# First transfers, first modulation column and planner margins of a fused transformer block, changed together

## The chip, the core and the metric

The kernel runs on one core of a Trainium2 chip. The core has a matrix engine (PE, which multiplies a 128x128 stationary tile with a moving tile of up to 512 columns), a vector engine (DVE), an activation engine (ACT), a general engine (POOL), and transfers that SP issues (DMA). The engines run side by side and wait for each other through semaphores. The metric is the device time of one execution in microseconds (us).

## The reference

One block works on x (1024 tokens of 1024 features) with a conditioning vector c, all in float32. Cut to what is computed:

```python
c_act = silu(c)
shift1, scale1, gate1, shift2, scale2, gate2 = split(c_act @ ada_w + ada_b, 6)
h = rmsnorm(x, norm1_g) * (1 + scale1) + shift1
u, v, val, gate = split(h @ w_in + b_in, 4)            # 512 columns each
y_a = gelu(u) * (causal_mix_in_chunks_of_128(layernorm(gelu(v))) + b_s)
y_b = silu(group_layernorm(causal_conv31(val * sigmoid(gate))))
x = x + gate1 * (concat(rmsnorm(y_a), rmsnorm(y_b)) @ w_out)
h2 = rmsnorm(x, norm2_g) * (1 + scale2) + shift2
g, up = split(h2 @ w_ffn_in, 2)                        # 2816 columns each
x = x + gate2 * ((silu(g) * up) @ w_ffn_out)
shift_f, scale_f = split(c_act @ ada_f_w + ada_f_b, 2)
out = rmsnorm(x, norm_f_g) * (1 + scale_f) + shift_f
```

## The kernel before

Features lie on the 128 partitions and tokens along the rows, so a feature block k (0 to 7) of x is a tile of 128 x 1024. The tokens are worked in two halves of 512. A product in float32 is made from three products of parts: each operand is split into a high part of shorter numbers and a low part with the rest, and `mm3` adds high x high (L750), low weight x high (L751) and high weight x low (L752). The high part is a copy by ACT and the low part a subtraction on DVE or POOL (L733 and L734 turn a weight `raw_k` into `wh_k` and `wl_k`). The FFN forms its products from seven sums of blocks (L1131 to L1139).

The columns of the modulation (scale, shift and gate; 64 columns of 128 features) are products of a 128 x 1024 piece of `ada_w` with silu(c), which stands in every partition of `cact`. DVE multiplies and sums a piece in one instruction (L703, SCALAR_TENSOR_TENSOR over 1024 elements, its sum read out behind it); some pieces go over POOL and ACT instead (L700, L701). `cact` is made at the start: PE spreads c over the partitions (L662), ACT takes silu (L663).

The start makes the norm's factor for the first half. As the blocks of x land, `first_rstd` squares them (L886 on DVE for odd k, L888 on ACT for even k), PE sums over the features (L890), ACT takes the root (L894), DVE the reciprocal (L895), and four matmuls with `sel_tok` spread the factors over the partitions (L897). `keep_busy` puts matmuls on a tile of zeros, `idle`, between these steps (L876). Then, for each k: two columns (scale, shift), the weight `wk[k]`, the scaled x `t_h` (L926), its modulated high part `h` (L928, ACT) and low part (L932, L933), and 24 products into eight PSUM tiles. The columns' pieces land in the tiles `ypad`, which the convolution uses later.

Behind that, for the first half: the products of u, v and the gated values (`glu`, L826); the convolution of 31 taps on DVE and POOL (`conv_pair`: `cv` at L1070 and L1073, its sum with POOL's part `s` at L1079); the chunk mixing, whose bias tile is `bst` (L860, from row sums `rs` that PE makes in a PSUM tile); the norms of both branches (`rt_a`, `rt_b`, L799); and w_out. The second half follows with the same steps, then the FFN, and last the final norm (L1442).

The order of instructions on each engine isn't that of the code. `fix_order` builds a graph of all steps with a cost for each, lists it forward by rank and backward, several times, and binds each engine to the resulting order. It makes 12 such orders (three pairs of factors by which steps and transfers are stretched, four rounds each) and keeps the one that `replay` finds best over jittered costs. `edges` are order constraints given by hand; one list of them holds the transfers of the first phase (`in_turn`).

## Time and profile before

| quantity | value |
| --- | --- |
| median of 3 runs | 964.54 us (963.92 to 966.73) |
| profiled execution | 967.9 us, its span 965.8 us |
| PE busy | 946.5 us (98%) |
| DVE busy | 861.9 us (89%) |
| ACT busy | 482.1 us (50%) |
| POOL busy | 413.6 us (43%) |
| granted clock of PE, mean | 0.995 |
| PE busy in the first 20 us | 15.03 us |
| PE busy from 120 to 140 us | 18.30 us, granted clock 0.91 |
| PE busy in the last 26 us | 16.69 us |

In the timeline a row has the start, the duration, the engine, the line, the operation, the tiles, and in brackets the idle time of the engine before it with what ended it. A row of several instructions has their number behind x and their whole time. In the list of waits a row names who waited, for whom, the total in us, the times and the longest. Matmuls overlap, so the time from one start to the next tells the pace of PE.

### The profile page before, as it was taken

To read this page: it belongs to the slowest core of one execution; us is meant where nothing else is said; L and a number is where in the kernel's file an instruction comes from. 1 tells how busy PE (TensorE), PEld (TensorE's weight loads), DVE (VectorE), ACT (ScalarE), POOL (GpSimd) and SP (SyncE) were. 2 spreads that over 40 slices of the span, in tenths; PEclk is the share of its full clock that TensorE was granted. 3 is DMA by queue.
4 is the path that set the end of the run, shared out by engine and by line. 5 is a ranking of instruction groups with operands and counts; after the bars stand their busy time and mean duration, and the time that the engine had idled before them with its cause. 6 is when DMAs were issued, how large, how long until landed. Compare 5 with 4: busy or idle time off the path is not lost.

```text
span 965.8 us, 12863 instructions
## 1 busy us (share of the span) xinstructions
PE 946.5 (98%) x4461; PEld 767.1 (79%) x4461; DVE 861.9 (89%) x1226; ACT 482.1 (50%) x770; POOL 413.6 (43%) x253
## 2 busy tenths in 40 slices
...
GB/s 351 325 265 136 110 174 88 153 159 130 139 280 202 147 146 138 263 205 119 239 238 251 221 236 243 249 236 238 224 171 277 269 158 260 164 33 165 54 1 174
DMA packets 70498, 184.24 MB, mean 191 GB/s; under 512 B 7841, under 2 KB 8353, under 8 KB 70434
## 3 DMA queue, kind: packets, MB, share of 16 engines
...
## 4 chain that ended last, share of the span: by engine, by line
PE 84%; DVE 9%; DMA 2%; ACT 2%; issue 2%; POOL 1%; SPq 0%; POOLq 0%; ACTq 0%; DVEq 0%
PE B L1139 31%; PE C L1139 18%; PE ah L1139 9%; PE A L1139 3%; PE po L752 3%; PE po L751 3%; PE po L750 3%; DVE cv L1070 2%; PE p L752 2%; PE p L750 2%; PE p L751 2%; PE v L750 2%; PE v L752 1%; DVE ada L703 1%; PE v L751 1%
## 5 line engine op out<-in xcount | busy, mean ns | idle before, releaser
L1139 PE MATMUL B<-h,w_f 128*128 128x512 f32 x816 | 189.9, 389 | 0.6 <-ACT w_f L1131 0.3
L1139 PEld LDWEIGHTS B<-h,w_f 128*128 128x128 f32 x816 | 153.1, 188 | 33.0 <-ACT w_f L1131 0.8
L1070 DVE SCALAR_TENSOR_TENSOR cv<-ypad,colt,cv 128x512 f32<-128x512 f32 x216 | 147.8, 745 | 0.3
L1139 PE MATMUL B<-fa,w_d 128*128 128x512 f32 x528 | 125.0, 389 | 0.0
L1139 PE MATMUL C<-h,w_f 128*128 128x512 f32 x528 | 123.7, 389 | 0.0
L1139 PEld LDWEIGHTS C<-h,w_f 128*128 128x128 f32 x528 | 99.1, 188 | 20.9 <-ACT w_f L1131 0.3
L1139 PEld LDWEIGHTS B<-fa,w_d 128*128 128x128 f32 x528 | 99.0, 188 | 20.9 <-DVE x L1500 0.3
L1139 PE MATMUL ah<-h,wh_a 128*128 128x512 f32 x320 | 101.3, 394 | 0.0
L1426 POOL TENSOR_TENSOR sq_nf<-sq_nf,sq_nf 128x512 f32<-128x512 f32 (+1 forms) x15 | 17.4, 1163 | 170.9 <-ACT sq_nf L1420 170.8
L1131 ACT ACTIVATE w_f<-raw_f 128x512 fp32r<-128x512 f32 x68 | 42.4, 630 | 87.8 <-PE B L1139 38.8
L734 POOL TENSOR_TENSOR wl_a<-raw_a,wh_a 128x1024 fp32r<-128x1024 f32 x20 | 49.4, 2468 | 77.0 <-ACT wh_a L733 77.0
L1131 ACT ACTIVATE w_d<-raw_d 128x512 fp32r<-128x512 f32 (+1 forms) x72 | 42.0, 593 | 80.2 <-PE B L1139 33.6
L1132 DVE TENSOR_TENSOR w_f<-raw_f,w_f 128x512 fp32r<-128x512 f32 x68 | 71.7, 1061 | 7.6 <-ACT w_f L1131 7.4
L1139 PEld LDWEIGHTS ah<-h,wh_a 128*128 128x128 f32 x320 | 59.8, 188 | 14.8 <-issue 1.7
L1383 POOL TENSOR_TENSOR x<-x,up 128x512 f32<-128x512 f32 x20 | 36.1, 1805 | 73.4 <-ACT x L1382 73.4
L1139 PE MATMUL C<-fa,w_d 128*128 128x512 f32 (+1 forms) x291 | 63.9, 370 | 0.0
L1139 PE MATMUL ah<-h,wl_a 128*128 128x512 f32 x160 | 62.3, 389 | 0.0
L1139 PEld LDWEIGHTS C<-fa,w_d 128*128 128x128 f32 x291 | 51.0, 188 | 9.2
L1132 DVE TENSOR_TENSOR fa<-a,fa 128x512 fp32r<-128x512 f32 x77 | 52.0, 712 | 1.1 <-ACT fa L1131 1.1
L1500 DVE SCALAR_TENSOR_TENSOR x<-B,cond,x 128x512 f32<-128x512 f32 x48 | 35.7, 746 | 18.0 <-PE B L1139 17.5
L1132 DVE TENSOR_TENSOR w_d<-raw_d,w_d 128x512 fp32r<-128x512 f32 (+1 forms) x72 | 50.6, 712 | 0.0
L1131 ACT ACTIVATE fa<-a 128x512 fp32r<-128x512 f32 x77 | 46.5, 626 | 7.4 <-DMA a<-acts 4.8
...
## 6 DMA issues: line engine op xcount, KB each, us to landing
...
```

What stands on the lines that cost most here:

```text
L703: V.scalar_tensor_tensor(raw, raw, 1.0, cact, op0=ALU.mult, op1=ALU.mult, accum_out=cond[:, j:j + 1])
L734: lo_eng.tensor_tensor(lo[:, cut], raw[:, cut], hi[:, cut].bitcast(F32), op=ALU.subtract)
L750: PE.matmul(acc, shi, mhi, start=start, stop=False)
L751: PE.matmul(acc, slo, mhi, start=False, stop=False)
L752: PE.matmul(acc, shi, mlo, start=False, stop=stop)
L1070: V.scalar_tensor_tensor(accs[j], src, wc, accs[j], op0=ALU.mult, op1=ALU.add)
L1131: A.activation(dst[:, 0, :], src, AF.Copy)
L1132: lo_eng.tensor_tensor(dst[:, 1, :], src, dst[:, 0, :].bitcast(F32), op=ALU.subtract)
L1139: last_mm = PE.matmul(bank[:, cols], s, m[:, cols], start=first and p == 0 and i == 0, stop=p == n - 1 and i == 2, skip_group_check=True)
L1383: G.tensor_tensor(g0, g0, up0, op=ALU.mult)
L1426: G.tensor_tensor(run, run, t, op=ALU.add)
L1500: V.scalar_tensor_tensor(x_tile(k, part), bank[:, cols], ccol(GATE2, k), x_tile(k, part), op0=ALU.mult, op1=ALU.add)
```

## The change

At the start it does the following.

- The transfers' order is pair 0 of x's blocks, c, the first 80 columns of the small constants `colt` (with c as eight columns in it), pairs 1 and 2, pair 3 as two halves, then the matrix for the first scale column, the piece for the first shift column, `wk[0]` in two halves, and the rest of `colt`. Before it was c, the four pairs, the two pieces, `wk[0]`, `colt`.
- The first scale column is made by PE: eight matmuls with the columns of silu(c) as stationary operand, a copy by ACT, and one matmul that sums the rows. The DVE step for it falls away.
- `gain` (one plus the bias, times the norm's gain) is made right after the first square instead of behind the first `t_h`.
- The squares of k = 1, 3, 4, 5 and 7 are on DVE, those of 0, 2 and 6 on ACT.
- The first `h` is made by DVE (TENSOR_SCALAR) instead of ACT.
- Ten matmuls on `idle`, 128x512, are added (nine stand ahead of the c matmuls in the order that comes out); the ones between the steps are now 32x128 and more of them (`IDLE`).
- The first steps of DVE, ACT and the transfers are bound to the written order by `edges`.

In the planner, the replay falls away. One pair of factors, (1.03, 1.1), two rounds, and ranks with a random term replace the 12 orders. With this the order moves a little in the whole program.

```diff
-IDLE = (1, 1, 2, 3, 3)
+IDLE = (4, 6, 6, 6, 4)
+WARM_UP = 10
+BY_VECTOR = (1, 3, 4, 5, 7)
...
-MARGINS = ((1.01, 1.05), (1.015, 1.075), (1.02, 1.1))
-JITTER = (0.008, 0.08)
-TRIALS = 4
+MARGIN = (1.03, 1.1)
+ROUNDS_OF_ORDER, SPREAD, SEED = 2, 0.05, 577509
...
-def jittered(g, order, seed):
+def fix_order(tc, edges, stacked, reusing):
 
     import random
-    rng = random.Random(seed)
-    with stretched(g, lambda s: 1 + abs(rng.gauss(0, JITTER[s.dma]))):
-        return replay(g, order)
-
-
-def fix_order(tc, edges, stacked, reusing, rounds=4):
-
+    rng = random.Random(SEED)
     g = Graph(list(tc.nc.cur_bb.bb.instructions), edges, stacked, reusing)
-    orders = []
-    for margin in MARGINS:
-        with stretched(g, lambda s: margin[s.dma]):
-            order, done, follows = forward(g, list(range(len(g.steps))))
-            for _ in range(rounds):
-                tail = backward(g, [-t for t in done], follows)
-                order, done, follows = forward(g, [-t for t in tail])
-                orders.append(order)
-    times = [sum(jittered(g, order, seed) for seed in range(TRIALS)) for order in orders]
-    best = orders[times.index(min(times))]
-    for steps in best.values():
+    with stretched(g, lambda s: MARGIN[s.dma]):
+        order, done, follows = forward(g, list(range(len(g.steps))))
+        for _ in range(ROUNDS_OF_ORDER):
+            tail = backward(g, [-t for t in done], follows)
+            order, done, follows = forward(g, [-(t + rng.gauss(0, SPREAD)) for t in tail])
+    for steps in order.values():
...
-    c_load = nc.sync.dma_start(c_row[0:1, :], c).ins
     colt = const.tile([P, NCOL], F32, name="colt")
     xs = [[const.tile([P, 2, H], F32, name=f"x{half}_{i}") for i in range(KD // 2)] for half in range(2)]
-    in_turn = [c_load] + [nc.sync.dma_start(xs[0][i], xT[0, i]).ins for i in range(KD // 2)]
+    early = _OFF["norm2_g"]
+    in_turn = [nc.sync.dma_start(xs[0][0], xT[0, 0]).ins, nc.sync.dma_start(c_row[0:1, :], c).ins,
+               nc.sync.dma_start(colt[:, 0:early], cols[:, 0:early]).ins]
+    in_turn += [nc.sync.dma_start(xs[0][i], xT[0, i]).ins for i in range(1, KD // 2 - 1)]
+    in_turn += [nc.sync.dma_start(xs[0][KD // 2 - 1][:, a, :], xT[0, KD // 2 - 1, :, a, :]).ins for a in range(2)]
...
+    cact_cols = colt[:, 0:KD]
+    A.activation(cact_cols, cact_cols, AF.Silu)
+    silu, on = [], dict(V=[], A=[])
     for h in range(2):
         cb = cv_bank(f"c{h}")
         PE.matmul(cb, ones[0:1].broadcast_to([1, P]), c_row[0:1, hs(h)], start=True, stop=True)
-        silu = A.activation(cact[:, hs(h)], cb, AF.Silu).ins
-    with issue_after(silu):
+        silu.append(A.activation(cact[:, hs(h)], cb, AF.Silu).ins)
+    with issue_after(silu[-1]):
...
-        nc.sync.dma_start(raw, src)
+        for i in range(parts):
+            cut = slice(i * 1024 // parts, (i + 1) * 1024 // parts)
+            nc.sync.dma_start(raw[:, cut], src[:, cut])
...
-            ins = PE.matmul(first_bank(3, 0), idle[:, 0:P], idle, start=True, stop=True).ins
+            ins = PE.matmul(first_bank(3, 0)[0:32, 0:P], idle[:, 0:32], idle[:, 0:P], start=True, stop=True).ins
...
-            if k % 2:
-                V.tensor_tensor(t, src, src, op=ALU.mult)
+            if k in BY_VECTOR:
+                on["V"].append(V.tensor_tensor(t, src, src, op=ALU.mult).ins)
             else:
-                A.activation(t, src, AF.Square)
+                on["A"].append(A.activation(t, src, AF.Square).ins)
+                if k == 0:
+                    on["A"] += silu
             for q in range(4):
                 mm = PE.matmul(bank[q * 32:(q + 1) * 32, 0:P], ones.broadcast_to([P, 32]),
                                t[:, q * P:(q + 1) * P], start=k == 0, stop=k == KD - 1).ins
             keep_busy(IDLE[k // 2] if k % 2 else 0, mm)
         rt = sb.tile([P, P], F32, tag="rt", name="rt_n1_0", bufs=2)
-        A.activation(rt, bank[:, 0:P], AF.Sqrt, bias=epst, scale=1.0 / D)
+        on["A"].append(A.activation(rt, bank[:, 0:P], AF.Sqrt, bias=epst, scale=1.0 / D).ins)
         last["rstd"] = V.reciprocal(rt, rt).ins
+        on["V"].append(last["rstd"])
         for q in range(4):
             mm = PE.matmul(bank[:, q * P:(q + 1) * P], sel_tok[:, q:q + 1].broadcast_to([P, P]),
                            rt, start=True, stop=True).ins
         keep_busy(IDLE[4], mm)
         return bank
 
+    for _ in range(WARM_UP):
+        PE.matmul(first_bank(3, 0), idle[:, 0:P], idle, start=True, stop=True)
     r1a_bank = first_rstd()
...
     gain = const.tile([P, KD], F32, name="gain")
+    V.scalar_tensor_tensor(gain, bcol(SCALE1, 0, KD), 1.0, colt[:, _OFF["norm1_g"]:_OFF["norm1_g"] + KD],
+                           op0=ALU.add, op1=ALU.mult)
+
+    def first_scale():
+
+        raw = ypad[0][:, HALO:HALO + D]
+        nc.sync.dma_start(raw, ada1)
+        bank = gn_bank("scale_rows")
+        for k in range(KD):
+            q = k % 4
+            PE.matmul(bank[q * 32:(q + 1) * 32, 0:P], cact_cols[:, k:k + 1].broadcast_to([P, 32]),
+                      raw[:, k * P:(k + 1) * P], start=k < 4, stop=k >= 4)
+        rows = sb.tile([P, P], F32, tag="rt", name="scale_rows", bufs=2)
+        on["A"].append(A.activation(rows, bank[:, 0:P], AF.Copy).ins)
+        PE.matmul(bank[:, P:P + 1], rows, sel_tok[:, 4:5], start=True, stop=True)
+        return bank[:, P:P + 1]
+
     for k in range(KD):
         n = len(nc.cur_bb.bb.instructions)
-        ada_cols(SCALE1 * 8 + k, dst=ypad[2 * k % 4][:, HALO:HALO + D])
-        with issue_after(last["rstd"]):
+        if k == 0:
+            first_scale_col = first_scale()
+        else:
+            ada_cols(SCALE1 * 8 + k, dst=ypad[2 * k % 4][:, HALO:HALO + D])
+        with issue_after(last["rstd"]) if k else nullcontext():
             ada_cols(SHIFT1 * 8 + k, dst=ypad[(2 * k + 1) % 4][:, HALO:HALO + D])
+        if k == 0:
+            behind = len(nc.cur_bb.bb.instructions)
+            t = tmp("t_h1_0_0")
+            on["V"].append(V.tensor_tensor(t, x_tile(0, hs(0)), r1a_bank, op=ALU.mult).ins)
         w_k = weights(wk[k], f"k{k}", V, parts=2 if k == 0 else 1)
-        scale, shift, weight = loads(n)
+        in_turn += loads(n)
         if k == 0:
-            in_turn += [scale, shift, weight, nc.sync.dma_start(colt, cols).ins]
-            V.scalar_tensor_tensor(gain, bcol(SCALE1, 0, KD), 1.0, colt[:, _OFF["norm1_g"]:_OFF["norm1_g"] + KD],
-                                   op0=ALU.add, op1=ALU.mult)
+            in_turn.append(nc.sync.dma_start(colt[:, early:], cols[:, early:]).ins)
+        scaled = A.activation(ccol(SCALE1, k), first_scale_col if k == 0 else ccol(SCALE1, k), AF.Identity,
+                              bias=gain[:, k:k + 1], scale=col("norm1_g", k)).ins
+        shifted = A.activation(ccol(SHIFT1, k), ccol(SHIFT1, k), AF.Identity, bias=bcol(SHIFT1, k)).ins
+        if k:
+            t = tmp(f"t_h1_0_{k}")
+            V.tensor_tensor(t, x_tile(k, hs(0)), r1a, op=ALU.mult)
+        h = h1[0][k] = act_tile(f"h1_0_{k}", 0)
+        if k == 0:
+            h_hi = V.tensor_scalar(h[:, 0, :], t, ccol(SCALE1, k), ccol(SHIFT1, k), op0=ALU.mult, op1=ALU.add).ins
         else:
-            in_turn += [scale, shift, weight]
-        A.activation(ccol(SCALE1, k), ccol(SCALE1, k), AF.Identity, bias=gain[:, k:k + 1], scale=col("norm1_g", k))
-        A.activation(ccol(SHIFT1, k), ccol(SHIFT1, k), AF.Identity, bias=bcol(SHIFT1, k))
-        t = tmp(f"t_h1_0_{k}")
-        V.tensor_tensor(t, x_tile(k, hs(0)), r1a_bank if k == 0 else r1a, op=ALU.mult)
-        h = h1[0][k] = act_tile(f"h1_0_{k}", 0)
-        h_hi = A.activation(h[:, 0, :], t, AF.Identity, bias=ccol(SHIFT1, k), scale=ccol(SCALE1, k)).ins
+            h_hi = A.activation(h[:, 0, :], t, AF.Identity, bias=ccol(SHIFT1, k), scale=ccol(SCALE1, k)).ins
         if k == 0:
-            with issue_after(h_hi):
-                A.activation(r1a, r1a_bank, AF.Copy)
+            on["V"].append(h_hi)
+            kinds = [[i for i in nc.cur_bb.bb.instructions[behind:] if i.engine == e and type(i).__name__ != "InstDMACopy"]
+                     for e in (nc.vector.engine, nc.scalar.engine)]
+            on["V"] += [i for i in kinds[0] if i not in on["V"]]
+            rounded = [i for i in kinds[1] if i not in (scaled, shifted)]
+            on["A"] += [scaled, *rounded[:1], shifted, *rounded[1:], A.activation(r1a, r1a_bank, AF.Copy).ins]
         A.activation(t, t, AF.Identity, bias=ccol(SHIFT1, k), scale=ccol(SCALE1, k))
         V.tensor_tensor(h[:, 1, :], t, h[:, 0, :].bitcast(F32), op=ALU.subtract)
         for j in range(4):
             for vg in range(2):
                 mm3(first_bank(j, vg), unit(w_k, 4 * vg + j), full(h), k == 0, k == KD - 1)
-    edges.extend((b.name, a.name) for a, b in zip(in_turn, in_turn[1:]))
+    for ins in (in_turn, on["V"], on["A"]):
+        edges.extend((b.name, a.name) for a, b in zip(ins, ins[1:]))
```

DVE at the start, before. `ypad` rows are columns (the first is the scale of k = 0, the second its shift), `wl_k` is the low part of a weight, and the last row is the low part of `h` of k = 0.

```order
L886 TENSOR_TENSOR sq_n_0_7_171<-x_3_78 128x512
L703 SCALAR_TENSOR_TENSOR ypad_108,cond<-ypad_108,cact 128x1024
L895 RECIPROCAL rt_n_0_180<-rt_n_0_180 128x128
L703 SCALAR_TENSOR_TENSOR ypad_109,cond<-ypad_109,cact 128x1024
L926 TENSOR_TENSOR t_h_0_0_208<-x_0_75,ssq_n_0_123 128x512
L919 SCALAR_TENSOR_TENSOR gain<-colt 128x8
L734 TENSOR_TENSOR wl_k_199<-raw_k_196,wh_k_198 128x512 x2
L703 SCALAR_TENSOR_TENSOR ypad_110,cond<-ypad_110,cact 128x1024
L933 TENSOR_TENSOR h_0_0_210<-t_h_0_0_208,h_0_0_210 128x512
```

DVE there, after:

```order
L850 TENSOR_TENSOR sq_n_0_7_200<-x_3_77 128x512
L861 RECIPROCAL rt_n_0_212<-rt_n_0_212 128x128
L665 SCALAR_TENSOR_TENSOR ypad_116,cond<-ypad_116,cact 128x1024
L907 TENSOR_TENSOR t_h_0_0_241<-x_0_74,ssq_n_0_141 128x512
L920 TENSOR_SCALAR h_0_0_255<-t_h_0_0_241,cond 128x512
L698 TENSOR_TENSOR wl_k_247<-raw_k_243,wh_k_246 128x512 x2
L931 TENSOR_TENSOR h_0_0_255<-t_h_0_0_241,h_0_0_255 128x512
```

The scale column and `gain` are gone from this stretch (`gain` stands five rows ahead of it), the first `h` (TENSOR_SCALAR) has come in, and the weight's low parts and the low part of `h` follow without a column between them.

PE in the products of k = 1, before (`h_0_1` is the block's `h`; L752 rows take its low part):

```order
L750 MATMUL p_0_215<-h_0_1_260,wh_k_252 128x512
L751 MATMUL p_0_215<-h_0_1_260,wl_k_253 128x512
L752 MATMUL p_0_215<-h_0_1_260,wh_k_252 128x512
L750 MATMUL p_1_219<-h_0_1_260,wh_k_252 128x512
L751 MATMUL p_1_219<-h_0_1_260,wl_k_253 128x512
L752 MATMUL p_1_219<-h_0_1_260,wh_k_252 128x512
L750 MATMUL p_0_223<-h_0_1_260,wh_k_252 128x512
```

PE there, after (L714, L715 and L716 are the lines L750, L751 and L752 of before):

```order
L714 MATMUL p_1_264<-h_0_1_305,wh_k_297 128x512
L714 MATMUL p_0_268<-h_0_1_305,wh_k_297 128x512
L714 MATMUL p_1_272<-h_0_1_305,wh_k_297 128x512
L715 MATMUL p_0_260<-h_0_1_305,wl_k_298 128x512
L715 MATMUL p_1_264<-h_0_1_305,wl_k_298 128x512
L715 MATMUL p_0_268<-h_0_1_305,wl_k_298 128x512
L715 MATMUL p_1_272<-h_0_1_305,wl_k_298 128x512
L714 MATMUL p_0_276<-h_0_1_305,wh_k_297 128x512
L715 MATMUL p_0_276<-h_0_1_305,wl_k_298 128x512
L714 MATMUL p_1_280<-h_0_1_305,wh_k_297 128x512
L715 MATMUL p_1_280<-h_0_1_305,wl_k_298 128x512
L716 MATMUL p_0_260<-h_0_1_305,wh_k_297 128x512
```

The low part of `h` was needed by the third product of the block; now it is needed by the 13th (one L714 row stands ahead of those shown).

DVE around `bst`, before. `ada` is a modulation column that DVE makes, `cv` are taps of the convolution, `s` the sums that close its first pair of blocks, and the `cv_2` and `cv_3` rows open the second pair.

```order
L1070 SCALAR_TENSOR_TENSOR cv_0_1214<-ypad_108,colt,cv_0_1214 128x512
L1070 SCALAR_TENSOR_TENSOR cv_1_1215<-ypad_109,colt,cv_1_1215 128x512
L1079 TENSOR_TENSOR s_0_1210<-s_0_1210,cv_0_1214 128x512
L1079 TENSOR_TENSOR s_1_1211<-s_1_1211,cv_1_1215 128x512
L1073 TENSOR_SCALAR cv_2_1530<-ypad_110,colt 128x512
L1073 TENSOR_SCALAR cv_3_1531<-ypad_111,colt 128x512
L860 SCALAR_TENSOR_TENSOR bst<-rs,colt,bst 128x128 x4
L1070 SCALAR_TENSOR_TENSOR cv_2_1530<-ypad_110,colt,cv_2_1530 128x512
L1070 SCALAR_TENSOR_TENSOR cv_3_1531<-ypad_111,colt,cv_3_1531 128x512
```

DVE there, after:

```order
L1069 SCALAR_TENSOR_TENSOR cv_1_1260<-ypad_116,colt,cv_1_1260 128x512
L1069 SCALAR_TENSOR_TENSOR cv_0_1259<-ypad_115,colt,cv_0_1259 128x512
L1069 SCALAR_TENSOR_TENSOR cv_1_1260<-ypad_116,colt,cv_1_1260 128x512
L824 SCALAR_TENSOR_TENSOR bst<-rs,colt,bst 128x128 x4
L1069 SCALAR_TENSOR_TENSOR cv_0_1259<-ypad_115,colt,cv_0_1259 128x512
L1069 SCALAR_TENSOR_TENSOR cv_1_1260<-ypad_116,colt,cv_1_1260 128x512
L1069 SCALAR_TENSOR_TENSOR cv_0_1259<-ypad_115,colt,cv_0_1259 128x512
L1069 SCALAR_TENSOR_TENSOR cv_1_1260<-ypad_116,colt,cv_1_1260 128x512
L1078 TENSOR_TENSOR s_0_1255<-s_0_1255,cv_0_1259 128x512
L1078 TENSOR_TENSOR s_1_1256<-s_1_1256,cv_1_1260 128x512
L1072 TENSOR_SCALAR cv_2_1575<-ypad_117,colt 128x512
L1072 TENSOR_SCALAR cv_3_1576<-ypad_118,colt 128x512
```

`bst` stood behind the first pair's last taps, its sums and the first taps of the next pair; now four taps of the first pair, the sums and those first taps all stand behind it.

42 lines of the change are left out of this document (6 added, 36 removed).

## Prediction

> **What bounds the kernel now.** I read the page first, then who waited for whom on PE, then the timeline of the two places where PE waits longest. PE is busy for 946.5 of 965.8 us, so whatever this change can win lies in the 19 us that are left and in stretches where the clock of PE is low.
>
> ```profile
> span 965.8 us, 12863 instructions
> PE 946.5 (98%) x4461; PEld 767.1 (79%) x4461; DVE 861.9 (89%) x1226; ACT 482.1 (50%) x770; POOL 413.6 (43%) x253
> ...
> PE c L662 <- DMA c_row<-c: 2.4, 1, 2.4
> PE v L750 <- DVE bst L860: 2.1, 1, 2.1
> ...
> PE p L750 <- ACT h L928: 1.7, 1, 1.7
> PE p L752 <- DVE h L933: 1.0, 1, 1.0
> ...
> PE pm L1013 <- DVE ya L1019: 0.8, 1, 0.8
> PE ssq_b L805 <- DVE rt_b L799: 0.6, 1, 0.6
> ```
>
> These are PE's waits (total, times, longest). The rows on c and h belong to the start, which the diff rewrites. The row on bst is a single wait in the middle, which no line of the diff names but which the new order of DVE moves. These are the start's steps in order of time (start, duration, engine, line):
>
> ```profile
> 1.01 0.27 DVE L864 MEMSET idle<- 128x256 uint32 x1
> 2.44 3.75 PE L662 MATMUL c<-c_row,ones 1*128 1x512 f32 x4 [2.44 <-DMA c_row<-c]
> 6.33 0.58 ACT L663 ACTIVATE cact<-c 128x512 f32<-128x512 f32 x1
> 6.93 1.28 ACT L665 ACT_TABLE_LOAD   x1
> ...
> 8.22 0.20 ACT L665 ACTIVATE warm<-epst 128x1 f32<-128x1 f32 x1
> 9.38 0.69 DVE L886 TENSOR_TENSOR sq_n<-x 128x512 f32<-128x512 f32 x1 [0.56 <-DMA x<-xT]
> 10.65 1.23 DVE L703 SCALAR_TENSOR_TENSOR ypad<-ypad,cact 128x1024 f32<-128x1024 f32 x1 [0.58 <-DMA ypad<-ada]
> 11.04 0.37 ACT L894 ACTIVATE rt_n<-ssq_n,epst 128x128 f32<-128x128 f32 x1 [1.04 <-PE ssq_n L890]
> 11.80 0.95 DVE L895 RECIPROCAL rt_n<-rt_n 128x128 f32<-128x128 f32 x1
> 14.00 0.69 DVE L926 TENSOR_TENSOR t_h<-x,ssq_n 128x512 f32<-128x512 f32 x1 [0.17 <-PE ssq_n L897]
> 15.41 0.81 ACT L928 ACTIVATE h<-t_h,cond 128x512 fp32r<-128x512 f32 x1
> 16.27 0.50 PE L750 MATMUL p<-h,wh_k 128*128 128x512 f32 x1 [1.66 <-ACT h L928]
> 18.86 1.89 DVE L926 TENSOR_TENSOR t_h<-x,r_n 128x512 f32<-128x512 f32 x3
> 20.67 1.22 DVE L734 TENSOR_TENSOR wl_k<-raw_k,wh_k 128x1024 fp32r<-128x1024 f32 x1
> 21.80 1.22 DVE L703 SCALAR_TENSOR_TENSOR ypad<-ypad,cact 128x1024 f32<-128x1024 f32 x1
> 22.95 0.68 DVE L933 TENSOR_TENSOR h<-t_h,h 128x512 fp32r<-128x512 f32 x1
> 23.68 0.50 PE L752 MATMUL p<-h,wh_k 128*128 128x512 f32 x1 [1.01 <-DVE h L933]
> ```
>
> What starts the real products is one chain: last part of x (9.38), square, sum, root, reciprocal (ends 12.75), t_h at 14.00, h by ACT to 16.22, PE at 16.27. The scale column's 1.23 us on DVE holds the reciprocal from 11.41 to 11.80. PE stops again at 23.68 for the low part of the second k-block; the next of these waits in time is the one for bst, near 120.
>
> The second place:
>
> ```profile
> 106.15 6.59 DVE L703 SCALAR_TENSOR_TENSOR ada<-ada,cact 128x1024 f32<-128x1024 f32 x1
> 106.90 4.76 POOL L734 TENSOR_TENSOR wl_v<-raw_v,wh_v 128x1024 fp32r<-128x1024 f32 x2
> 112.67 5.36 DVE L1070 SCALAR_TENSOR_TENSOR cv<-ypad,colt,cv 128x512 f32<-128x512 f32 x8
> 117.94 1.27 DVE L1079 TENSOR_TENSOR s<-s,cv 128x512 f32<-128x512 f32 x2
> 119.13 1.39 DVE L1073 TENSOR_SCALAR cv<-ypad,colt 128x512 f32<-128x512 f32 x2
> 120.44 1.11 DVE L860 SCALAR_TENSOR_TENSOR bst<-rs,colt,bst 128x128 f32<-128x128 f32 x4
> 121.70 0.47 PE L750 MATMUL v<-wh_v,h 128*128 128x512 f32 x1 [2.12 <-DVE bst L860]
> ...
> 123.19 0.63 PE L752 MATMUL v<-wl_v,h 128*128 128x512 f32 x1
> 123.62 0.63 PE L750 MATMUL v<-wh_v,h 128*128 128x512 f32 x1
> 126.11 0.39 PE L750 MATMUL v<-wh_v,h 128*128 128x512 f32 x1
> 126.34 0.40 PE L751 MATMUL v<-wh_v,h 128*128 128x512 f32 x1
> 124.00:126.00 2.00, 2.00 (x6) 1.56 (x5) 2.00 (x4) 0.38 (x2) 2.00 (x2) 0.50 0.42 152
> L703 DVE SCALAR_TENSOR_TENSOR ada<-ada,cact x12: 1211/1914/6586, 49.0 to 199.1; 128x1024 f32<-128x1024 f32 x12
> ```
>
> One column product on DVE (alone 1.21, here 6.59 us) lasts until POOL's two neighbours are done. It makes bst 5.4 us late, PE waits 2.12 us for it, and after the pause the matmuls come at 0.43 us apart (123.19 to 123.62) where they come at 0.23 otherwise (126.11 to 126.34); the granted clock is 0.50 in the windows' row (its last columns: clock, DMA share, GB/s). About nine matmuls run so, 9 x 0.20 = 1.8 us. The place costs 2.1 + 1.8 = 3.9, say 4 us.
>
> **The change part by part.** The sum is made against the profiled execution, 967.9 us (965.8 and 2.1 around it); it stands 3.4 above the median of 964.54. I carry the difference over to the median.
>
> *Start of the chain.* Call the end of the reciprocal R (12.75 before). The column's 1.23 us leaves DVE, and the reciprocal can follow the root: with x landing as before, 9.38 and 0.69 for the last square, 0.97 to the root (10.07 to 11.04), and 0.37 + 0.95 and a hand-over (1.36 together) give R = 12.4. That is one end. The other comes from c, now the second transfer and behind nine warm-up matmuls on PE. They start about 1.3, when `idle` is set, and at 0.43 us they end at 5.2; the c matmuls then take 3.75 if slow, 1.9 if at full clock. Behind them ACT has silu 0.58, a square (as DVE's, 0.69), the table 1.28 + 0.20 and the square of k = 6, 0.69: 3.44 in all, then the 0.97 and 1.36. Full clock from the first gives 5.2 + 1.9 + 5.8 = 12.9; slow throughout gives 14.7. In the middle place the pitch was back 4.4 us after PE resumed (121.70 to 126.11), which here is 5.7: c done at about 7.4 and R = 13.1. I take R = 13.0, between the two near rows.
>
> The Trainium skill, "TensorE: Matmul & The Clock Gate", Part 1, says that the clock opens after a free-running 3.4 us window of sustained work. By it the opening would be anywhere from 4.7 to 8.1 (estimate), so R from 12.9 to 14.3; the 4.4 us of this trace lies within that.
>
> *From R to the 37th product.* t_h starts R + 1.25 as now. The first column of scale comes from PE, nine small matmuls, eight of them ahead of the ones that spread R's factors. Their matrix takes the queue place of the one that landed at 10.65, 2.4 us before R, and PE only waits between the last sum and R: cost nothing; a later landing would hold t_h by as much. `gain` is made early, where DVE waits for x, and the small copies on ACT lie beside the second column: nothing. On DVE then follow t_h 0.60, h 0.70 (a row as L1073's; between 0.6 and ACT's 0.81), two halves of wl 1.13, h's low part 0.60, a column 1.15, t_h 0.60, a column 1.15, three t_h 1.81, wl 1.13, a column 1.15, h's low part 0.68 (distances of the rows 18.86 to 22.95): 10.7. The second low part is ready at R + 11.95, later than now after R (10.88), since DVE took over h. But the new order puts 12 products of k = 1 ahead of this wait instead of two, so it is the 37th product that waits. Before, the 27th began at 23.68 and the 37th ten pitches later, 25.95. The gain is 25.95 - (R + 12.0) = 13.95 - R: 0.95 us at R = 13.0, between -0.75 and +1.55. The first products come about R + 2.6 = 15.6, 0.7 earlier; what PE waits later is this second wait. Further k-blocks need 4.7 to 5.3 us of DVE against 24 x 0.227 = 5.4 of PE: no further loss.
>
> *The middle.* bst now stands ahead of the last four convolution steps, both sums and the two TENSOR_SCALARs: 4 x 0.67 + 1.27 + 1.39 = 5.3 us less ahead of it. Two more columns (2.3) stand ahead of it, and a step of 1.4 has moved in front of the first glu, where DVE has room: 4.4 net. PE reaches the place 1 us earlier. bst would be done at 121.6 - 1 - 4.4 = 116.2 at equal blocking, against 118.6 for PE: the wait of 2.1 goes, and the slow clock with it, -4.0. If blocking adds over 2.4 us, part is back.
>
> *What is given back.* Up to the end of the first half's mixing DVE is full, and at the waits for ya and rt_b (0.8 and 0.6) PE is already held by it. The order gives DVE as much work as before to the end of the convolution (within 1.5 us either way by the same durations), so DVE gains the start, 1 us, and the 5.4 only if that block doesn't return elsewhere. I take these two waits over again, 1.4 of the 5.0, as lost there; bounds 0 (DVE gains both) and 4.0 (the start alone). The FFN, from about 445, has PE full and the same steps; the tail differs by one or two moved steps: 0, within 0.3. Sum: -0.95 - 4.0 + 1.4 = -3.55, so 964.35 for a profiled execution and 961.0 for the median.
>
> **The rivals.** (a) *Start only:* the middle doesn't pay, since DVE's queue takes it back or the timed runs never had that stall (the 3.4 us between profile and median would be it): 964.54 - 0.95 = 963.6. For: the stall is nearly 3.4. Against: the order is fixed, and the three runs lie within 2.8 us.
>
> (b) *The warm-ups delay c:* R = 14.7, the start loses 0.75 instead of winning 0.95: 962.7 with the rest as above. The row for it is the 3.75 us of c, all slow after nothing; against it the 4.4 us to full clock.
>
> (c) *Slower: a second blocked column.* DVE's rt_b has a column two rows ahead of it in the new order, and POOL works there on pairs of weights, as here:
>
> ```profile
> 203.56 4.76 POOL L734 TENSOR_TENSOR wl_o<-raw_o,wh_o 128x1024 fp32r<-128x1024 f32 x2
> 208.24 0.94 DVE L799 RECIPROCAL rt_b<-rt_b 128x128 f32<-128x128 f32 x1
> ```
>
> Say that the column at 106 is held again, now behind bst, and this one too, for 5.4 us each. PE is 5 us ahead there; DVE has gained 1 us of start and 4.3 of work that the new order puts behind rt_b (by the same durations), and loses 5.4: it is 0.1 late. PE waits 0.6 + 5.0 + 0.1 = 5.7, and the slow clock adds 1.8: 7.5 lost against 5.0 won, +2.5, so 967.0. It decides from about 3 us of blocking. By the Trainium skill, "SBUF — State Buffer", Who interferes with whom, whichever of the two engines starts first holds the shared port pair for its whole instruction; the 6.59 against 1.21 agrees, and by that rule any meeting can do so. Against it: by the row above, half of the twelve such columns ended within 1.9 us.
>
> (d) *The order does nothing for the middle and the start is equal:* within 1 us of 964.5; it needs R = 13.9 and the block again. Little speaks for both.
>
> **How the numbers follow.** Forecast (start about 1 us earlier, middle's stall gone, part given back) 0.45: 958.5 to 962.0 is its own range. (a) 0.22, (b) 0.08, (c) 0.20, (d) 0.05. A change within 0.3% (2.9 us, 961.6 to 967.4) can hardly be told from none. Faster takes nine tenths of the forecast and a little of (a) and (b), 0.43; slower takes two thirds of (c), whose price may well be higher with two such places, and a little of (b), 0.15; the rest is 0.42. The range reaches from 958.5 to 967.5.
>
> **What would show it.** After: the first real matmul near 15.6 and a wait of about 1 us before the 37th; the reciprocal near 13.0, with the last c matmul at about 7.4; no wait of v for bst, and a granted clock of 1.00 near 125; PE's waits for ya and rt_b longer by about 1.4 in sum. I am wrong if c ends near 9, if a column on DVE of 4 us or more is followed by a PE wait, or if PE starts later than 16.3.

## Result and the profile after

The changed kernel takes 962.04 us (median of 19 runs, 961.35 to 964.31) beside 966.49 us of the kernel before on the same chip (median of 19, 963.77 to 969.1): a ratio of 0.9961, 95% interval 0.9951 to 0.9971, so faster by 0.39%. Neither set of times is one heap (a group of times with a gap to the next). The changed kernel's lie at 961.35 to 962.2 (11 runs) and 963.82 to 964.31 (8), those of before at 963.77 to 965.62 (9) and 966.49 to 969.1 (10). The profiled execution after, 963.87 us with a span of 962.1, is of the upper heap; so was that of before (967.9). The medians of the lower heaps are 961.9 and 964.5, 2.6 us apart; how many runs fall in which heap moves the median, and with it the ratio.

PE's waits after, from the view of waits (total, times, longest):

```profile
PE ssq_nf L1443 <- DVE rt_nf L1441: 1.6, 1, 1.6
PE p L870 <- DVE epst L609: 1.3, 1, 1.3
PE p L714 <- DVE h L920: 1.1, 1, 1.1
PE pm L1012 <- ACT ada L663: 1.0, 1, 1.0
PE ssq_n L864 <- DVE rt_n L861: 0.7, 1, 0.7
PE p L715 <- DVE wl_k L698: 0.6, 1, 0.6
```

The waits for `bst`, `ya` and `rt_b` are gone, not longer; a new one of 1.0 (`pm` for a modulation column on ACT) has come. The start, from the timelines of PE and DVE, in order of time:

```profile
1.28 4.02 PE L870 MATMUL p<-idle 128*128 128x512 bf16 x9 [1.28 <-DVE epst L609]
5.24 3.78 PE L624 MATMUL c<-c_row,ones 1*128 1x512 f32 x4
8.94 1.08 PE L856 MATMUL ssq_n<-sq_n,ones 128*32 128x128 f32 x16
...
11.68 0.69 DVE L850 TENSOR_TENSOR sq_n<-x 128x512 f32<-128x512 f32 x1 [1.24 <-ACT warm L627]
14.67 0.95 DVE L861 RECIPROCAL rt_n<-rt_n 128x128 f32<-128x128 f32 x1 [2.30 <-ACT rt_n L860]
18.49 0.96 PE L714 MATMUL p<-h,wh_k 128*128 128x512 f32 x3 [1.11 <-DVE h L920]
24.86 1.22 DVE L698 TENSOR_TENSOR wl_k<-raw_k,wh_k 128x1024 fp32r<-128x1024 f32 x1
26.13 1.20 PE L715 MATMUL p<-h,wl_k 128*128 128x512 f32 x4 [0.57 <-DVE wl_k L698]
27.14 0.69 DVE L931 TENSOR_TENSOR h<-t_h,h 128x512 fp32r<-128x512 f32 x1
28.09 1.52 PE L716 MATMUL p<-h,wh_k 128*128 128x512 f32 x6
```

Nine warm-ups and then four passes for c, all at the slow pace (3.78 us; 1.98 at full pace, below), end at 9.0. ACT loads its table behind them, and the last square starts at 11.68 (before: 9.38). R, the end of the reciprocal, is 15.62 (before: 12.75), the first product comes at 18.49 (16.27), the 37th at 28.09 (26.09 by the timeline of before; the prediction reckoned 25.95). This start is 2.0 us slower, not 0.95 faster. The middle:

```profile
106.97 3.54 POOL L1064 TENSOR_TENSOR s<-s,cp 128x512 f32<-128x512 f32 x2
107.24 2.13 DVE L665 SCALAR_TENSOR_TENSOR ada<-ada,cact 128x1024 f32<-128x1024 f32 x1
115.23 1.11 DVE L824 SCALAR_TENSOR_TENSOR bst<-rs,colt,bst 128x128 f32<-128x128 f32 x4
116.95 2.40 POOL L698 TENSOR_TENSOR wl_v<-raw_v,wh_v 128x1024 fp32r<-128x1024 f32 x1 [0.46 <-ACT wh_v L697]
124.00:126.00 2.00, 2.00 (x10) 1.69 (x9) 2.00 (x4) 2.00 (x4) 2.00 (x2) 1.00 0.02 4
```

The column took 2.13 us where it took 6.59, `bst` was done at 116.3, and the windows' row for 124 to 126 (its last columns are clock, DMA share and GB/s) has the clock at 1.00 instead of 0.50.

To see where time went, I cut the span at two events that every version has: the start of `rs` (PE sums rows for `bst`) and the first product of `po`, the output of w_out, with `y_b`. The rows before and after:

```profile
L858 PE MATMUL rs<-wt,ones x4: 592/618/643, 107.4 to 107.9; 128*64 128x512 f32 x4
L750 PE MATMUL po<-y_b,wh_o x64: 389/389/397, 215.9 to 383.7; 128*128 128x512 f32 x64
```

```profile
L822 PE MATMUL rs<-wt,ones x4: 592/618/643, 109.2 to 109.7; 128*64 128x512 f32 x4
L714 PE MATMUL po<-y_b,wh_o x64: 389/389/389, 213.3 to 380.9; 128*128 128x512 f32 x64
```

The same cut for all kernels that were profiled (us; the names are those of the experiments below; "middle" is from `rs` to `po`, "rest" from there to the end of the span):

| kernel | first product | `rs` | middle | rest | span |
|---|---|---|---|---|---|
| before | 16.27 | 107.4 | 108.5 | 749.9 | 965.8 |
| b_bst_first | 16.43 | 107.5 | 108.4 | 750.5 | 966.4 |
| b_mid | 16.28 | 107.9 | 107.8 | 749.9 | 965.6 |
| b_col_early4 | 16.40 | 108.0 | 112.1 | 749.8 | 969.9 |
| b_col_late | 17.52 | 108.6 | 104.6 | 750.4 | 963.6 |
| b_new_planner | 17.50 | 110.3 | 103.2 | 750.1 | 963.6 |
| a_old_planner | 18.51 | 111.6 | 102.3 | 754.2 | 968.1 |
| after | 18.49 | 109.2 | 104.1 | 748.8 | 962.1 |
| a_bst_late | 16.20 | 107.0 | 104.5 | 748.8 | 960.3 |
| a_c_first | 16.32 | 107.1 | 104.1 | 749.0 | 960.2 |
| a_no_warm | 17.34 | 108.1 | 104.1 | 748.8 | 961.0 |
| a_c_pe | 18.96 | 109.8 | 104.1 | 748.7 | 962.6 |
| a_tall | 16.28 | 106.9 | 104.1 | 748.8 | 959.8 |
| a_tall_late | 20.23 | 110.9 | 104.1 | 748.8 | 963.8 |

Between the two profiles the stretch up to `rs` lost 1.8, the middle won 4.4, and the rest won 1.1: together the 3.7 between the spans.

The ratios below are to before as it was run beside each kernel. Of before's runs, 9 of 19, 5 of 18, 12 of 35, 4 of 23 and 1 of 10 lay in the lower heap, so a ratio of one round can't be set against that of another to the last tenths of a per cent; the medians of the changed kernels tell more.

### The profile page after: what moved, and what is told of

Same layout as the page of the kernel before. It is cut to its first block, busy times and chain, and to the rows that moved or that the text cites. A ratio compares the mean times of both kernels' runs of the same rounds, so it can differ in the third digit from the quotient of the medians.

```text
span 962.1 us, 12964 instructions
## 1 busy us (share of the span) xinstructions
PE 948.1 (99%) x4505; PEld 769.8 (80%) x4505; DVE 856.2 (89%) x1230; ACT 483.9 (50%) x772; POOL 405.9 (42%) x253
## 4 chain that ended last, share of the span: by engine, by line
PE 95%; DVE 2%; ACT 2%; issue 0%; ACTq 0%; DVEq 0%
PE B L1138 32%; PE C L1138 19%; PE ah L1138 11%; PE A L1138 4%; PE po L716 3%; PE po L714 3%; PE po L715 3%; PE p L715 3%; PE p L714 3%; PE p L716 3%; PE pu L715 2%; PE pu L716 2%; PE pu L714 2%; PE v L714 1%; PE v L716 1%; PE v L715 1%
## 5 line engine op out<-in xcount | busy, mean ns | idle before, releaser
L1131 DVE TENSOR_TENSOR w_f<-raw_f,w_f 128x512 fp32r<-128x512 f32 x68 | 74.1, 1094 | 1.4 <-ACT w_f L1130 1.3
L1385 POOL TENSOR_TENSOR x<-x,u 128x512 f32<-128x512 f32 x22 | 35.8, 1629 | 74.2 <-DVE u L1384 74.2
L1131 DVE TENSOR_TENSOR w_d<-raw_d,w_d 128x512 fp32r<-128x512 f32 (+1 forms) x72 | 47.5, 669 | 0.8 <-ACT w_d L1130 0.7
```

What stands on the lines that cost most here:

```text
L1131: lo_eng.tensor_tensor(dst[:, 1, :], src, dst[:, 0, :].bitcast(F32), op=ALU.subtract)
L1385: G.tensor_tensor(g1, g1, u2, op=ALU.mult)
```

## Experiments on the middle

Names with b_ start from the kernel before, those with a_ from the changed one. A step is moved after the planner has made its order: `move` takes it out of its engine's list and puts it in front of another step (with `True`: behind it). So all other rows stay.

**bst alone, both ways.** b_bst_first puts it ahead of the first pair's last four taps:

```diff
+                    if (half, jp, tap, j) == (0, 0, CW - 2, 0):
+                        MOVES.append((last["bst"], ins.name))
```

> The kernel before, with one edit: the four DVE steps of the mixing bias stand ahead of the last four convolution steps of the first pair, as in the changed kernel, instead of behind the pair's sums and the next pair's first two taps; all else stands in its old order. My theory (the wait for the bias near 120 us and the slow clock after it cost 4 us): the wait goes, the granted clock stays at full from 120 to 128, and 0 to 1.4 us of it come back at the waits for DVE that follow, so the time falls by 2.6 to 4.0 us, ratio to before 0.9959 to 0.9973. Rival (DVE is full, so the same time is lost at its next late step): the wait reappears within the first half's mixing and the ratio is within 0.999 and 1.001.

Measured: 967.45 us, ratio 0.9992 [0.9975, 1.001], as the rival had it, though the waits that came were others. The wait for `bst` was gone, and PE waited elsewhere:

```profile
PE v L768 <- POOL wl_v L750: 1.8, 1, 1.8
PE v L766 <- ACT vn L991: 1.4, 1, 1.4
106.31 6.58 DVE L719 SCALAR_TENSOR_TENSOR ada<-ada,cact 128x1024 f32<-128x1024 f32 x1
116.80 2.41 POOL L716 TENSOR_TENSOR ada<-ada,cact 128x1024 f32<-128x1024 f32 x1 [4.99 <-DVE bst L876]
```

The column took 6.58 us here as well. Until it ends, its buffer isn't free for the piece that POOL multiplies next (SP waited 6.6 us for it and issued that load at 112.92), POOL sat idle for 4.99 us ahead of that product, and `wl_v` stands behind it. a_bst_late puts `bst` back behind the sums and the first steps of the next pair:

```diff
+                    if (half, j) == (0, 3):
+                        MOVES.append((last["bst"], ins.name, True))
```

> The changed kernel, with one edit: the four DVE steps of the mixing bias stand behind the pair's sums and the next pair's first two taps, as before; all else as changed. In the changed kernel's trace they ended at 116.3, and 5.2 us of DVE work moves ahead of them, so they end near 121.5, and PE reaches the products that need their tile at 121.3 in the profiled execution: a wait of about 0.2 to 0.5 us there, and in executions whose start is 2 us shorter a wait of 2.3 us and perhaps the slow clock. My theory: 0.5 to 4 us slower than the changed kernel, ratio to before 0.997 to 1.0. Rival (where the bias stands is of no account, the column held by POOL made it): no wait, ratio 0.996 as the changed kernel.

Measured: 962.12 us, ratio 0.9949 [0.993, 0.9967], five runs at 961.7 to 962.31 and two at 964.41 and 964.71; PE waited 0.2 for `bst`, the middle took 104.5. So in these two profiles the place of `bst`, on which my price for the middle rested, is worth 0.1 us with a held column and 0.4 without.

**POOL's and ACT's order.** b_mid has, besides b_bst_first, one move on POOL (`product24` is the modulation product in question) and one on ACT (`sum24` is its sum):

```diff
+    MOVES.append(([LAST["wl_v_2"], LAST["wl_v_3"]], LAST["product24"]))
...
+                if j == 25:
+                    MOVES.append(([last["sum24"]], last["sum25"]))
```

> The kernel before with three moves and nothing else: bst four convolution steps earlier on DVE, the third and fourth wl_v of v ahead of the modulation product that stood between them on POOL, and that product's sum behind the next steps on ACT. The modulation column near 106 stays where it was on DVE. Theory (the order around POOL made the middle): with bst alone moved, PE stopped 1.8 us for wl_v instead; with these moves both waits go, v's last products start some 2 to 3 us earlier than at 176.0, and 2 to 4 us are won at the end: ratio 0.996 to 0.998. Rival (the blocked column itself, or DVE's whole work, is the bound): the waits move on to vn near 170 and to ya or rt_b near 200, and under 1 us is won: ratio over 0.999.

Measured: 968.92 us, ratio 1.0024 [1.0011, 1.0036], so slower. In its profile the column happened to get through, which the next part is about:

```profile
106.62 1.86 DVE L722 SCALAR_TENSOR_TENSOR ada<-ada,cact 128x1024 f32<-128x1024 f32 x1
107.35 5.73 POOL L753 TENSOR_TENSOR wl_v<-raw_v,wh_v 128x1024 fp32r<-128x1024 f32 x2
PE gn L1118 <- ACT s L1115: 2.9, 1, 2.9
```

POOL's modulation products now came later by a piece of `wl_v` or two, ACT in its fixed order waited 2.87 us for the first and 0.7 to 1.4 for most of the next, and its `vn` and `s` stand among these sums: PE waited 2.9 for `s`, which it does not in the kernel before. Both expectations missed this: taking waits away by hand made a new one, and it hides what the free column was worth here.

**The column.** b_col_early4 moves only the column of DVE near 106, four steps forward; b_col_late only the same column, eight steps back, to where POOL has run out of work (8 in place of -4):

```diff
+    column = LAST["column23"]
...
+            i = names.index(column)
+            steps.insert(i + (-4), steps.pop(i))
```

> The kernel before with one move: the modulation column near 106 four convolution steps (2.7 us) earlier on DVE; all else in place, so bst, POOL and ACT keep their order. Theory (the blocked column is the cause): the column then meets only a part of POOL's row of instructions and takes at most 4 us instead of 6.6; bst is done 2.5 us or more earlier, its wait of 2.1 goes, the column's buffer is free sooner, so the load of POOL's modulation product starts before 110 instead of at 112.8 and no wait for wl_v follows; 2 to 4 us are won, ratio 0.996 to 0.998. Rival (a column that starts while POOL has instructions queued is passed over until POOL runs dry, near 111.7): it takes about 9 us, all stays as late as before, ratio 0.999 to 1.001.

> The kernel before with one move: the modulation column near 106 eight convolution steps later on DVE, to about 111.5, where POOL has nothing to run until its next modulation product has been loaded. All else is in place; the column's buffer comes free at about 112.7, as in the profile of before, so that load stays late. The times of the kernel before lie in two groups (964.0 to 965.7 and 966.8 to 970). Theory (they differ by who wins the contest for the column, and its 5.4 us on DVE are what costs): the column takes 1.2 to 1.5 us in every run, bst is done near 114, no wait for bst, and the times form one group near 964.5 with none above 966.5; ratio 0.996 to 0.998. Rival 1 (the late load of POOL's product costs as much): no wait for bst, but 1.5 to 2 us for wl_v near 126 in every run, one group near 967.5. Rival 2 (the groups have another cause): both groups stay.

b_col_early4: median 965.76, ratio 1.0014 [0.9992, 1.0036], not told apart from before; but its 12 times are two heaps, 964.2 to 966.0 (7) and 970.7 to 972.6 (5). The profiled one is of the upper:

```profile
104.11 9.22 DVE L725 SCALAR_TENSOR_TENSOR ada<-ada,cact 128x1024 f32<-128x1024 f32 x1
107.46 4.79 POOL L756 TENSOR_TENSOR wl_v<-raw_v,wh_v 128x1024 fp32r<-128x1024 f32 x2
PE v L772 <- DVE bst L882: 4.8, 1, 4.8
```

POOL ran four instructions, from 103.86 to 112.25, before the column ended at 113.3; PE then waited 4.8 for `bst`, and the middle took 112.1. The rival's mechanism is there in the profiled run, and the lower heap of 7 speaks for its absence in the others, which neither expectation said.

b_col_late: 964.67 us, all 12 runs between 963.66 and 965.6, ratio 0.9972 [0.9961, 0.9982].

```profile
108.13 4.78 POOL L756 TENSOR_TENSOR wl_v<-raw_v,wh_v 128x1024 fp32r<-128x1024 f32 x2
112.66 1.33 DVE L725 SCALAR_TENSOR_TENSOR ada<-ada,cact 128x1024 f32<-128x1024 f32 x1
116.43 1.11 DVE L882 SCALAR_TENSOR_TENSOR bst<-rs,colt,bst 128x128 f32<-128x128 f32 x4
```

One row moved, and the upper heap of before's times is gone, as the theory had it (no run of 12 against 19 of 23 beside it). Rival 1 was not put to the test: I had taken the load of POOL's product to stay late, but it was issued at 110.58, where before had it at 112.77. The middle took 104.6, against 108.5 of before and 104.1 of the changed kernel. So freeing the column wins 3.9 us in before's order, and the changed order, where it is free as well, wins 4.4; that the one is the reason of the other is inferred from the sizes, since no run holds the column in the changed order. There the column stands beside two `s` steps of POOL, and POOL has to wait for ACT (whose step starts at 108.32) between them; in that gap the column gets in, in all seven profiles of that order with 2.09 to 2.14 us.

What a held column waits for can be read off the rows: POOL's gapless row ends at 111.66 in before, 111.81 in b_bst_first and 112.25 in b_col_early4, and the column ends 1.08 us later each time (112.74, 112.89, 113.33), about as long as it takes alone (1.21).

**The planner's settings alone, and the start alone.** b_new_planner is before with the new settings, a_old_planner the reverse:

```diff
-MARGINS = ((1.01, 1.05), (1.015, 1.075), (1.02, 1.1))
...
+MARGIN = (1.03, 1.1)
...
```

> The kernel before with the changed planner settings alone (one pair of factors, two rounds, random term, no replay); the start's steps are those of before. The order it gives has bst ahead of the first pair's last taps on DVE, but on POOL the modulation products stand between the pieces of wl_v as before. Theory (the settings make better orders): the middle wins some 4 us and the end another 1, as in the changed kernel: ratio 0.994 to 0.996. Rival (what was won is a matter of a few rows that this order does not have): PE waits for wl_v or bst by 1.5 us or more near 125 and the ratio is 0.998 to 1.002.

> The changed kernel's start with the planner settings of before (three pairs of factors, four rounds, replay). Theory (the settings make the gain): the start is worth between -0.2 and +2.1 us by the other runs, the middle is as before, so ratio 0.999 to 1.003. Rival (the gain is a matter of rows around the middle, whatever the settings): in this order bst stands behind the sums and the modulation products stand between the pieces of wl_v, so the same 0.999 to 1.003 would come with waits for bst or wl_v of 1.5 us or more near 125; if those waits are absent and the time is still as before, the settings act elsewhere.

b_new_planner: 964.28 us, one heap (963.9 to 965.6), ratio 0.9972 [0.9961, 0.9983].

```profile
110.14 4.78 POOL L687 TENSOR_TENSOR wl_v<-raw_v,wh_v 128x1024 fp32r<-128x1024 f32 x2
112.01 3.99 DVE L656 SCALAR_TENSOR_TENSOR ada<-ada,cact 128x1024 f32<-128x1024 f32 x1
```

Its column is late, at 112.01, where POOL's row is nearly over, and took 3.99 us, again to 1.08 us behind POOL's end at 114.92, with `bst` right behind it; PE did not wait for `bst`. The gain equals that of b_col_late, between my two expectations. a_old_planner: 968.68 us, ratio 1.0 [0.9985, 1.0015], in two heaps, 965.5 to 966.33 (5 runs) and 968.66 to 970.09 (7). Its column took 1.21 us and its middle is the shortest of all, 102.3; it lost 2.4 us up to `rs` and 5.4 in the rest against the changed kernel, from the same start. So the settings have no fixed worth: with before's start the new ones win 0.28%, with the changed start they win more, and what the old settings' order loses in the rest is not shown.

## Experiments on the start

**Warm-ups.** a_no_warm makes all ten warm-ups 32 x 128; a_c_first puts c first in the transfers, its matmuls ahead of the warm-ups, and leaves three of these at full size (a_no_warm has 0 in place of 3; the last two lines are of a_c_first only).

```diff
-        PE.matmul(first_bank(3, 0), idle[:, 0:P], idle, start=True, stop=True)
...
+        if i < 3:
+            ins = PE.matmul(first_bank(3, 0), idle[:, 0:P], idle, start=True, stop=True).ins
+        else:
+            ins = PE.matmul(first_bank(3, 0)[0:32, 0:P], idle[:, 0:32], idle[:, 0:P], start=True, stop=True).ins
...
+    MOVES.append((spread, warmed[0]))
+    MOVES.append(([in_turn[1].name], in_turn[0].name))
```

> The changed kernel, with the ten warm-up matmuls 32x128 wide instead of 128x512, in the same places; all else in the same order. The c matmuls then start when c lands, about 4.3, instead of 5.24. If the warm-ups do nothing for the clock in time (theory from the profiled execution), c ends near 8.1, the reciprocal near 14.7 and the times are about 0.9 us below the slower group of the changed kernel's times (963.9), in one group. If they speed up c in the executions of the faster group (961.9; 11 of 19), the faster group is gone and the median is 1 us above the changed kernel's, 963.0. Ratio to before 0.9965 in either case; the groups tell them apart.

> The changed kernel, with c as the first transfer again and the two matmuls that spread c ahead of the warm-ups on PE; of the ten warm-ups three stay 128x512, seven are 32x128 wide. My theory (c behind the warm-ups is late: its matmuls ran from 5.24 to 9.0, all slow, and the reciprocal ended at 15.6 instead of the 13.0 forecast): the c matmuls start near 2.4, the last square of ACT ends near 10.1, the reciprocal near 12.5, the first product near 15.4 instead of 18.5, and the time falls by 1 to 3 us against the changed kernel, ratio to before 0.993 to 0.995. Rival (the reciprocal is bound by the transfers of x and the start's gain is lost at DVE later): reciprocal still after 14 or ratio 0.996.

Measured: 962.36 us (961.66 to 962.83), ratio 0.9945 [0.9926, 0.9964], and 962.14 us (962.0 to 962.59), ratio 0.9944 [0.9925, 0.9963]; each is one heap. The first product came at 17.34 and 16.32, R was 14.47 and 13.45. For a_no_warm both expectations gave 963.0, so neither is borne out; c first took the upper heap away, but it doesn't beat the lower heap of the changed kernel, and R = 12.5 was not reached. The profile of a_bst_late is of the lower heap, so it shows the changed start when it goes well:

```profile
4.91 1.98 PE L640 MATMUL c<-c_row,ones 1*128 1x512 f32 x4
6.82 0.64 PE L872 MATMUL ssq_n<-sq_n,ones 128*32 128x128 f32 x16
...
8.15 1.08 PE L872 MATMUL ssq_n<-sq_n,ones 128*32 128x128 f32 x16
8.00:12.00 4.00, 4.00 (x70) 3.15 (x69) 2.15 (x4) 2.24 (x5) 0.00 (x0) 0.58 1.03 397
```

So the two heaps of the changed kernel fit two outcomes of one thing: PE reaches full pace before the matmuls of c (1.98 us, first product 16.20) or not (3.78 us, 18.49). And full pace is lost again at 8.15: the same 16 passes take 1.08 instead of 0.64, and the windows' row has a granted clock of 0.58. The upper heap stays with this start: 8 of 19 runs of the changed kernel, 2 of 7 of a_bst_late and 7 of 12 of a_old_planner lie in it, while the five kernels with another start (this part and the next ones) have one heap each in 35 runs together.

**c as columns from PE.** a_c_pe is a_c_first with eight one-row matmuls in place of the early transfer of `colt`, which goes behind x; it has two full warm-ups instead of three, and `gain` is made ahead of the reciprocal.

```diff
+            ins = PE.matmul(c_bank[:, P + k:P + k + 1], c_row[0:1, k * P:(k + 1) * P], ones[0:1, 0:1], start=True, stop=True).ins
...
+    MOVES.append(([in_turn[2].name], in_turn[6].name, True))
```

> The changed kernel with its start in another order, all later rows of all engines in place: c is the first transfer and its products over the partitions come first on PE, c as columns comes from eight 1 x 128 matmuls on PE instead of the early transfer of colt, so that this transfer stands behind x, two warm-ups of 128 x 512 are left, and gain is made ahead of the reciprocal. Theory (the early transfer of colt held the blocks of x back by 1.3 us, and the end of the reciprocal sets all that follows): the last square starts near 9.4 instead of 10.7 (with c first) or 11.7 (profiled), the reciprocal ends at 12.1 to 12.4, the first product starts near 15.1, and the end is 1 us earlier than with c first alone: median 960.8 to 961.3, in one group, ratio 0.992 to 0.994. Rival (the piece for the first scale column then lands too late, or DVE has the start's work to do anyway): the first product no earlier than 16, and the times as with c first, 962.1, ratio 0.9944.

Measured: 964.4 us, ratio 0.9972 [0.9964, 0.9981]: worse than with c first, and by neither theory. The blocks of x did come sooner (DVE's squares at 4.64, 5.91 and 7.37; with c first at 4.65, 7.94 and 9.23), but PE was not ready for them:

```profile
6.05 3.41 PE L903 MATMUL ssq_n<-ones,c_row 1*128 1x1 f32 x16
```

Sixteen passes of one number each took 0.21 us apiece, and R was 16.09.

**One row or 128.** In a_c_first and a_c_pe the pace doubled near 10.1 and 13.4, about 4 us after the first matmul over 128 rows (6.21, 9.39), though PE had been busy with one-row matmuls since 2.5. The kernel before shows the same: PE was busy without a gap from 2.44, first with one-row matmuls and from 6.12 over 128 rows, and its pace doubled only between these rows:

```profile
9.00 1.08 PE L890 MATMUL ssq_n<-sq_n,ones 128*32 128x128 f32 x16
10.33 0.64 PE L890 MATMUL ssq_n<-sq_n,ones 128*32 128x128 f32 x16
```

a_tall tests that: c lies in four rows of a zeroed tile, and its matmuls go over all 128.

```diff
+    EXTRA[nc.gpsimd.memset(c_row[:, 0:2 * P], 0.0).ins.name] = None, False
...
-        PE.matmul(cb, ones[0:1].broadcast_to([1, P]), c_row[0:1, hs(h)], start=True, stop=True)
+            mm = PE.matmul(cb[:, q % 2 * 2 * P:(q % 2 + 1) * 2 * P], sel_tok[:, q:q + 1].broadcast_to([P, P]), c_row[:, 0:2 * P],
+                           start=True, stop=True).ins.name
```

> The changed kernel with one thing altered: c is spread over the partitions by matmuls over 128 rows (c lies in four rows, the other rows are set to zero by POOL first, four matmuls of 256 columns instead of two of 512 over one row); the start's other steps and all later rows stay. The four other profiles say that PE's pace doubles about 4 us after matmuls over 128 rows begin, and that the one-row matmuls of c do not count: it doubled 3.9 us after the first 128-row matmul with c first, 4.6 with no warm-ups, 4.0 with c as columns, and in the profile of the changed kernel not until after 12. Theory (rows in use decide): the matmuls of c take at most 3 us together in every run, PE keeps the doubled pace through the sums of squares, the second group of the changed kernel's times (near 964) is gone: one group at 961 to 962, reciprocal ending by 13.3; ratio 0.993 to 0.995. Rival (how the warm-ups fall against a clock of its own decides): both groups stay, some runs near 964.

Measured: 961.85 us, five runs between 961.49 and 961.9, ratio 0.993 [0.9918, 0.9943].

```profile
1.57 3.33 PE L907 MATMUL p<-idle 128*128 128x512 bf16 x8 [1.57 <-DVE epst L639]
4.74 1.89 PE L655 MATMUL c<-c_row,sel_tok 128*128 128x256 f32 x8
...
8.20 0.64 PE L893 MATMUL ssq_n<-sq_n,ones 128*32 128x128 f32 x16
12.37 0.95 DVE L898 RECIPROCAL rt_n<-rt_n 128x128 f32<-128x128 f32 x1 [0.95 <-ACT rt_n L897]
```

The matmuls of c take 1.89, the pace is not lost at 8.20, and no run lies near 964. That is what the theory says; but five low runs would also come up 6 times in 100 by a chance of 11 in 19 each, so the one heap alone is weak, and it is the kept pace that speaks for it, in one profile. The rival isn't ruled out, for rows in use are not all: with before's start the pace doubled near 10.1 to 10.8 in four profiles, but in b_col_late (whose rows follow) and b_new_planner only after 12, some 8 us after the first matmul over 128 rows at 6.00, and there the first product came 1.1 us later (17.5):

```profile
10.99 1.08 PE L912 MATMUL ssq_n<-sq_n,ones 128*32 128x128 f32 x16
12.00 1.89 PE L898 MATMUL p<-idle 128*128 128x512 bf16 x4
```

So what sets the moment stays open. a_tall is the fastest kernel of this study, though not told apart from the lower heap of the changed kernel.

**The same with colt behind x.** a_tall_late takes c as columns from two matmuls over 128 rows; c is the first transfer, and four full warm-ups stand ahead of its matmuls.

```diff
+    turned = [PE.matmul(c_bank[:, P + 4 * h:P + 4 * h + 4], c_row[:, h * P:(h + 1) * P], sel_tok[:, 0:4],
+                        start=True, stop=True).ins.name for h in range(2)]
```

> The same, and c as columns comes from two matmuls on PE, so that the early transfer of colt stands behind x; c is the first transfer, four warm-ups of 128 x 512 stand ahead of its matmuls, six become 32 x 128, gain is made ahead of the reciprocal. Theory (with PE at full pace the landing of x is the bound, and the early transfer of colt held it back by about 1.3 us): last square near 9.5 instead of 10.7, PE reaches it without a backlog, reciprocal ends by 12.6, first product near 15.5, the end about 1 us earlier than in the better group of the changed kernel: median 960.3 to 961.3, ratio 0.991 to 0.994. Rival (PE or the piece for the scale column is the bound): reciprocal at 13 or later and a median of 961.5 or more.

Measured: 965.16 us, ratio 0.9971 [0.9953, 0.9989]. The edit has a flaw of its own: silu(c) as columns is still written into `colt`, whose early part the transfer overwrites, so ACT had to wait for the transfer that I had just put last, and PE, whose sums share the PSUM tile, for ACT:

```profile
10.05 0.18 ACT L653 ACTIVATE colt<-ssq_n 128x8 f32<-128x8 f32 x1 [2.26 <-DMA colt<-cols]
16.31 0.95 DVE L903 RECIPROCAL rt_n<-rt_n 128x128 f32<-128x128 f32 x1 [2.99 <-ACT rt_n L902]
```

Whether x's landing is the next bound stays open. But a_tall and a_tall_late show what the start is worth, since all behind it is alike (104.1 and 748.8 in the table): R is 13.32 and 17.26, the span 959.8 and 963.8. A us of start is a us at the end.

## Why the prediction was right, and where it was not

The total was right for the ratio (961.0 of 964.54 is 0.9963, measured 0.9961) and 1.0 us low against the median. Between the two profiles it was nearly exact: 3.55 us forecast, 3.7 measured. That is luck in part, for the terms under it were off by up to 3 us, in both directions.

- *Start, -0.95: wrong sign in the profile, about zero in the good case.* The step "c done at about 7.4 and R = 13.1" failed. In the profile c ended at 9.0, as "slow throughout" had it, and R was 15.62, beyond the 14.7 that went with it. ACT's steps behind c took what the sum gave them (the last square ended at 12.37, forecast 3.44 behind c); it is the way from there to the root that took 1.90 us instead of 0.97, since the sums of squares ran at the slow pace too and PE had fallen behind with them. In the good case (a_bst_late) c ended at 6.9 and R was still 13.32: there ACT's last square waited for x until 9.99, and the one of DVE started at 10.67 (before: 9.38). The early transfer of `colt` stands ahead of these blocks, which "with x landing as before" left out (second pair of x at 5.80 before, 7.35 after, 5.91 in a_c_pe with `colt` behind x). The slow case is the mechanism of rival (b) and more of it. I had named it as the sign of being wrong "if c ends near 9", and "if PE starts later than 16.3"; in the profiled run both came.

```profile
9.99 0.63 ACT L868 ACTIVATE sq_n<-x 128x512 f32<-128x512 f32 x1 [0.38 <-DMA x<-xT]
```

- *Full clock 4.4 us after PE starts: from the wrong rows.* The 4.4 us to full clock came from the middle, where PE resumed with matmuls over 128 rows. The start of before, which was at hand, shows PE busy from 2.44 and at the slow pace until after 10: nearly 8 us.
- *From R to the 37th product, R + 12.0: size right (12.47), wait wrong.* PE did not stop at the 37th, for the low part of `h`: that was ready at 27.83, ahead of 28.09. It stopped at the 29th, for `wl_k`, which ended at 26.08. The prediction's own durations put `wl_k` at R + 10.1 and PE at its first use at about R + 9.0, so the wait could have been forecast; that the 37th comes out near R + 12 either way is chance.
- *Middle, -4.0: right size (-4.4), wrong lever.* I put the gain down to `bst` standing 4.4 us further ahead. By a_bst_late and b_bst_first its place is worth 0.4 at most. What pays is that the column is held for 2.13 instead of 6.59 us; moving that row alone (b_col_late) gives 3.9 in before's order. "At equal blocking" took the hold as fixed, and the hold was the term that mattered. `bst` was done at 116.3, forecast 116.2, but from a start 1.8 us later and a hold 4.5 us shorter.
- *Given back, +1.4: not there.* In b_col_late the waits for `ya` and `rt_b` stay at 0.7 and 0.6 and 3.9 us are won all the same: DVE carried the whole gain as far as these waits, the lower bound of this term. In the changed order both waits are gone; which rows do that, I have not tested.
- *Rest, 0 within 0.3: -1.1.* All kernels with the changed order take 748.7 to 749.0 there, those with before's order 749.8 to 750.5 (the two with the planner's settings swapped, 750.1 and 754.2, have orders of their own). It repeats to a few tenths and so belongs to the order; which rows make it, I have not tested.
- *The base.* I carried 3.4 us between profile and median through as a constant. Before's times lie in two heaps, 31 of 105 runs in the lower one over all rounds, and moving the column leaves only that one (b_col_late). So it is likely that the lower runs don't have the held column, though none of them was profiled. Rival (a), "the timed runs never had that stall", was then half true. Against the median of its round b_col_late wins 2.7 us (967.37 to 964.67), not 4, and in the comparison of medians the start's miss was made up by before's later runs, which lay higher than the three that I was shown.
- *Rival (c), a second held column,* did not occur: the twelve columns `ada` after took 1.19 to 2.77 us. By the rule that is cited there from the Trainium skill, "SBUF — State Buffer", Who interferes with whom, whichever engine starts first holds the shared port pair. Of an instruction that waits, the rows show more: POOL's next ones pass it over as well (two in before and three in b_col_early4, behind the one that ran when it came) or none does (b_mid, at the same place in the same order of rows as in before).
